# The last feed-forward of a two-layer diffusion transformer takes the residual times the norm's weights as its operand; the tokens' factors scale its up-product, and the shift is one more moving column

## The chip, the cores and the metric

The kernel runs on one core of a Trainium2 chip. A core has a matrix engine (TensorE, in the rows PE, its weight loads PEld), a vector engine (VectorE, DVE), a scalar engine (ScalarE, ACT), GpSimd (POOL) and queues that issue transfers (SP and others). Each engine works through its own queue in order and waits on semaphores for the others. Matrix products go to PSUM banks, which DVE and ACT read; everything else lies in SBUF. The metric is the time of one execution on the device, in microseconds (us).

## What is computed

There are 256 tokens and 256 context tokens of width 1024, two layers, each of a feed-forward, an attention block and a second feed-forward, all with a root-mean-square norm that is scaled and shifted by modulations. In the second layer the context's tokens end with the attention, so that its second feed-forward, the last one, has the 256 tokens alone:

```python
def _rmsnorm(x, g):
    y = x32 * lax.rsqrt(jnp.mean(x32 * x32, axis=-1, keepdims=True) + EPS)
    return (y * g.astype(jnp.float32)).astype(x.dtype)

def _modulate(h, shift, scale):
    return h * (1 + scale) + shift

def _swiglu(h, w_up, w_down):
    a, b = jnp.split(h @ w_up, 2, axis=-1)
    return (jax.nn.silu(a) * b) @ w_down

def _half_ffn(h, g, shift, scale, gate, w_up, w_down):
    return h + 0.5 * gate * _swiglu(_modulate(_rmsnorm(h, g), shift, scale), w_up, w_down)
...
        h_x = h_x + mod_x[:, :, 5] * (jnp.concatenate([o_a, o_b, o_c], axis=-1) @ w_out[l])
        h_x = _half_ffn(h_x, norm_g[l, 2], mod_x[:, :, 6], mod_x[:, :, 7], mod_x[:, :, 8], ffn2_up[l], ffn2_down[l])
```

The inner width is 2816, that is 22 chunks of 128 columns in each of the two halves a and b of the up-product.

## The kernel before

**Layout.** The residual `hT` has features on partitions: 8 chunks (index k) of 128 features, the tokens along the free dimension. Every operand of a large product is split into two float32r parts, a high part (a rounded copy) and a low part (the rest); a product is three matmuls, high by high, high by low, low by high (`mm3`, L348 to L350). An operand tile of the `act` pool (two buffers) holds both parts of all 8 chunks.

**Weights.** A stream of weight blocks comes by DMA into raw buffers (three). Each block gives two slots. `emit_split` makes a slot's high part on ACT (L306, 128x1024, or 128x768 for a part of six chunks) and its low part on DVE (L309). Seven slot buffers exist; `pump` keeps up to six or seven slots split ahead, and a next split is emitted after each slot is used up (`done`).

**Order.** Nothing reorders the program: it is emitted in the order in which each engine runs it. A clock of emitted TensorE work (`tick`, `later`) says where small steps are put among the large products: `AFTER` gives the delay of a norm's statistic and of what follows it, `ACC_LAG` that of the sums of squares.

**The boundary in question.** The second layer's `w_out_phase` calls `proj_out`: four slots of two chunks each. For every chunk of the result, DVE adds it, gated, to the residual (`resid`, L461), ACT squares it (L374) and DVE adds the squares up (L380, a chunk's sum emitted a little later). When the last chunk is out, `stat` sums over partitions by eight small matmuls (L409) and takes the reciprocal root by Newton's steps on DVE (L388 to L397); `spread` brings the tokens' factors to every partition through TensorE (L416) into PSUM; `apply` makes each chunk of the next operand from residual, weights, factors and shift:

```python
DVE.scalar_tensor_tensor(out=t, in0=hT[:, k, cols], scalar=gsc[:, i, k, v:v + 1], in1=rb[:, 0:TX], op0=ALU.mult, op1=ALU.mult)   # L436
ACT.activation(out=acol(a, k, v * TX, v * TX + TX)[0], in_=t, func=AF.Identity, bias=modT[:, l * 72 + 3 * n * 8 + k, v:v + 1])   # L437
DVE.scalar_tensor_tensor(out=al, in0=ts.pop(k), scalar=sh, in1=ah.bitcast(F32), op0=ALU.add, op1=ALU.subtract)                   # L431
```

In the second layer `flush()` emits all of that right behind `w_out_phase`, before the first product of the last feed-forward.

**The last feed-forward.** `ffn` goes through `FPARTS`, three parts of 8, 6 and 8 inner chunks. For each inner chunk there is a slot for a and one for b, 24 matmuls of 128x256 each, into a PSUM bank of its own (five banks rotate). In the first part the first four slots go together, chunk by chunk of the operand (`by_halves`). `up_evac` takes a pair of banks to a chunk of `g`, the operand of the down-product:

```python
ACT.activation(out=s[:, 0:n], in_=pa[:, 0:n], func=AF.Silu)                             # L552
DVE.tensor_tensor(out=u[:, 0:n], in0=s[:, 0:n], in1=pb[:, 0:n], op=ALU.mult)            # L555
ACT.copy(out=gh, in_=uv)                                                                # L558
DVE.tensor_tensor(out=gl, in0=uv, in1=gh.bitcast(F32), op=ALU.subtract)                 # L559
```

The silu is emitted behind the product of a, ahead of the weight split that follows it; the other three behind the product of b. After the ups of a part, `proj_out` runs eight down-slots of one output chunk each, which go through `g` chunk by chunk (24 matmuls; 18 in the part of six). In the last part each output chunk is also squared for the final norm and scaled into the result (`last_chunk`, L1265).

## Time and profile before

| what | value |
|---|---|
| time, median of three runs | 1739.68 us |
| lowest, highest | 1738.67 us, 1740.33 us |
| span of the profiled execution | 1741.7 us |
| mean granted TensorE clock | 0.987 |
| PE, DVE, ACT busy | 98%, 59%, 38% of the span |
| mean transfer rate | 142 GB/s |

The profile is of one execution, and its page gives no time of that execution other than its span from the first to the last instruction, 2.0 us above the median of the runs. Busy shares are means over stages with different limits. Matmuls overlap, so that a row's duration (0.28 us for 128x256) is longer than the distance from one to the next, and a busy PE says little about a slow one: the granted clock has to be read beside it. In a timeline row stand start, duration, engine, line, operation, result and operand, the shape, how many in a row, and in brackets the idle time of the engine before it with what ended it.

### The profile page before, as it was taken

The page shows a single profiled execution, that of the slowest core. Times are in us where ns is not written, and L with a number is a line of the kernel's source. Part 1 is how long each engine was busy: PE and PEld are TensorE (multiplying, and loading weights), DVE is VectorE, ACT ScalarE, POOL GpSimd, SP SyncE. Part 2 cuts the span into 40 slices and gives each one's busy share as a digit, 9 for nine tenths or more (in the row PEclk, how much of TensorE's full clock was granted, in tenths as well). Part 3 has the DMA queues.
Part 4 walks back from the last instruction along what each step waited for, and adds up shares of the span by engine and source line. Part 5 has one row for each costly group of instructions (what it writes and reads, how often), then busy time and mean ns, then how long its engine had stood idle before and what let it go on. Part 6 is the DMA issues. An engine that isn't in the chain of part 4 may idle for free.

```text
span 1741.7 us, 23662 instructions
## 1 busy us (share of the span) xinstructions
PE 1706.1 (98%) x9512; PEld 1428.7 (82%) x9512; DVE 1025.0 (59%) x1748; ACT 664.8 (38%) x1087; POOL 33.3 (2%) x48
## 2 busy tenths in 40 slices
PE   6999999999999999999999999999999999989998
PEld 4778888889886688888888898888888987789998
DVE  5666676566545586666664466545433656565554
ACT  4431322324545644323333243223222356554443
POOL 0000200000000000000000000020000000000000
PEclk8999999999999999999999999999999999989999
DMA  9755555431304325544653335455533133546561
GB/s 316 207 175 168 155 179 173 151 121 49 109 25 160 107 73 168 164 140 140 192 152 122 92 88 183 150 160 174 146 97 97 49 110 146 169 133 205 164 201 50
DMA packets 295335, 246.48 MB, mean 142 GB/s; under 512 B 9377, under 2 KB 262442, under 8 KB 293176
## 3 DMA queue, kind: packets, MB, share of 16 engines
q1 hardware_dynamic: 292680, 241.30, 44.7%
q0 software_dynamic: 1088, 2.15, 0.5%
q8 instruction: 75, 1.23, 0.3%
q10 hardware_dynamic: 1456, 1.52, 0.3%
q14 instruction: 36, 0.29, 0.1%
HBM read 243.88 MB, written 2.00 MB: 141 GB/s over the span
## 4 chain that ended last, share of the span: by engine, by line
PE 90%; DVE 4%; DMA 2%; ACT 2%; issue 1%; SPq 0%; DVEq 0%; ACTq 0%
PE mm L348 27%; PE mm L350 27%; PE mm L349 27%; PE mm L839 2%; PE mm L912 1%; PE aux L878 1%; PE mm L838 1%; DVE w L309 1%; PE ada L181 1%; DMA ada_raw<-in_w_ada_dram 1%; DVE ada_acc L221 1%; PE ada L229 1%; DMA raw<-in_w_ada_dram 1%; ACT w L306 1%; PE aux L409 0%
## 5 line engine op out<-in xcount | busy, mean ns | idle before, releaser
L348 PE MATMUL mm<-act,w 128*128 128x512 f32 (+1 forms) x2592 | 913.0, 352 | 5.6 <-ACT act L437 3.3
L350 PE MATMUL mm<-act,w 128*128 128x512 f32 (+1 forms) x2592 | 904.2, 349 | 1.8 <-DVE w L309 1.8
L349 PE MATMUL mm<-act,w 128*128 128x512 f32 (+1 forms) x2592 | 904.5, 349 | 1.0 <-DVE act L431 0.9
L348 PEld LDWEIGHTS mm<-act,w 128*128 128x128 f32 x2592 | 494.1, 191 | 89.3 <-issue 19.4
L350 PEld LDWEIGHTS mm<-act,w 128*128 128x128 f32 x2592 | 494.0, 191 | 64.1 <-DVE w L309 2.4
L349 PEld LDWEIGHTS mm<-act,w 128*128 128x128 f32 x2592 | 494.3, 191 | 62.5 <-DVE act L431 1.7
L309 DVE TENSOR_TENSOR w<-raw,w 128x1024 fp32r<-128x1024 f32 (+1 forms) x312 | 371.0, 1198 | 245.6 <-ACT w L306 245.2
L306 ACT CAST w<-raw 128x1024 fp32r<-128x1024 f32 (+1 forms) x312 | 314.9, 1023 | 120.4 <-PE mm L350 93.6
L221 DVE SCALAR_TENSOR_TENSOR ada_acc<-ada_raw,sc,ada_acc 128x512 f32<-128x512 f32 x308 | 216.0, 746 | 47.9 <-DMA ada_raw<-in_w_ada_dram 24.7
L558 ACT CAST act<-gf 128x512 fp32r<-128x512 f32 (+1 forms) x87 | 49.7, 571 | 318.7 <-DVE gf L555 318.7
L461 DVE SCALAR_TENSOR_TENSOR hT<-mm,hgt,hT 128x256 f32<-128x256 f32 x168 | 75.1, 480 | 97.8 <-PE mm L350 97.6
L552 ACT ACTIVATE sil<-mm 128x512 f32<-128x512 f32 (+1 forms) x87 | 47.6, 547 | 214.8 <-PE mm L350 214.5
L555 DVE TENSOR_TENSOR gf<-sil,mm 128x512 f32<-128x512 f32 (+1 forms) x87 | 54.3, 625 | 94.0 <-PE mm L350 77.7
L559 DVE TENSOR_TENSOR act<-gf,act 128x512 fp32r<-128x512 f32 (+1 forms) x87 | 54.9, 631 | 55.5 <-ACT act L558 55.5
L374 ACT ACTIVATE sq<-hT 128x256 f32<-128x256 f32 (+1 forms) x52 | 25.5, 492 | 108.4 <-DVE hT L461 108.4
L437 ACT ACTIVATE act<-nt,modT 128x256 fp32r<-128x256 f32 x88 | 43.4, 507 | 49.3 <-DVE nt L436 49.2
L219 ACT ACTIVATE ada_acc<-ada_raw,sc 128x512 f32<-128x512 f32 x44 | 29.6, 718 | 47.4 <-DMA ada_raw<-in_w_ada_dram 36.7
L855 DVE TENSOR_REDUCE nm<-mm 128x1 f32<-128x512 f32 (+1 forms) x60 | 41.0, 686 | 7.9 <-PE mm L839 7.2
L863 ACT ACTIVATE P<-mm,nm,rq 128x512 f32<-128x512 f32 (+1 forms) x48 | 33.7, 707 | 22.3 <-DVE nm L860 21.0
L431 DVE SCALAR_TENSOR_TENSOR act<-nt,modT,act 128x256 fp32r<-128x256 f32 x88 | 41.3, 480 | 1.3 <-ACT act L437 1.3
L436 DVE SCALAR_TENSOR_TENSOR nt<-hT,gsc,aux 128x256 f32<-128x256 f32 x88 | 40.8, 476 | 1.8 <-PE aux L416 1.2
L886 ACT COPY PT<-aux 128x512 f32<-128x512 f32 x60 | 32.2, 588 | 16.9 <-PE aux L878 12.9
(154 smaller groups left out, 885.5 us busy)
## 6 DMA issues: line engine op xcount, KB each, us to landing
raw<-in_ffn_up_dram SPq DMA_DIRECT2D x172, 512.0 KB
ada_raw<-in_w_ada_dram SPq DMA_DIRECT2D x192, 256.0 KB
raw<-in_ffn_down_dram SPq DMA_DIRECT2D x32, 1024.0 KB
raw<-in_w_ada_dram SPq DMA_DIRECT2D x16, 1024.0 KB
raw<-in_ffn_down_dram SPq DMA_DIRECT2D x16, 768.0 KB
raw<-in_w_in_dram SPq DMA_DIRECT2D x10, 1024.0 KB
raw<-in_w_out_dram SPq DMA_DIRECT2D x8, 1024.0 KB
raw<-in_w_ada_dram SPq DMA_DIRECT2D x12, 512.0 KB
```

Source lines behind the costliest of these rows:

```text
L221: DVE.scalar_tensor_tensor(out=o, in0=raw, scalar=col, in1=o, op0=ALU.mult, op1=ALU.add)
L306: ACT.copy(out=wh, in_=sl)
L309: DVE.tensor_tensor(out=wl, in0=sl, in1=wh.bitcast(F32), op=ALU.subtract)
L348: PE.matmul(out=ps, lhsT=wh, rhs=ah, start=start and i == 0, stop=False)
L349: PE.matmul(out=ps, lhsT=wh, rhs=al, start=False, stop=False)
L350: PE.matmul(out=ps, lhsT=wl, rhs=ah, start=False, stop=stop and i == last)
L437: ACT.activation(out=acol(a, k, v * TX, v * TX + TX)[0], in_=t, func=AF.Identity, bias=modT[:, l * 72 + 3 * n * 8 + k, v:v + 1])
L461: DVE.scalar_tensor_tensor(out=hT[:, k, cols], in0=ps, scalar=gate[:, k, v:v + 1], in1=hT[:, k, cols], op0=ALU.mult, op1=ALU.add)
L552: ACT.activation(out=s[:, 0:n], in_=pa[:, 0:n], func=AF.Silu)
L555: DVE.tensor_tensor(out=u[:, 0:n], in0=s[:, 0:n], in1=pb[:, 0:n], op=ALU.mult)
L558: ACT.copy(out=gh, in_=uv)
L559: DVE.tensor_tensor(out=gl, in0=uv, in1=gh.bitcast(F32), op=ALU.subtract)
```

## The change

The up-product of the last feed-forward is linear in its operand, and a token's factor is the same for all features. So the operand becomes the residual times the norm's weights (`gsc`), without factor and shift; the product of a token's column is multiplied by its factor afterwards; and the shift, which is the same for all tokens, is one more column of the operand, so that its product with the weights comes out as column 256 and is added as a bias. A second extra column is zero. `plain_operand` replaces `boundary` there, `last_ffn` replaces `ffn`; the `flush()` between them is dropped, and the first four slots are no longer taken together. `proj_out` and `w_out_phase` get a parameter `first`, called for each chunk between `resid` and `acc_chunk`. All other differences of the two files are comments and line numbers (one line more up to L480, five more up to L597, 91 more behind).

```diff
+NX = TX + 2
...
-    def proj_out(src, kl, ppair, gate, both, final, after, each=None):
+    def proj_out(src, kl, ppair, gate, both, final, after, each=None, first=None):
...
                 if final:
+                    if first:
+                        first(ppair * i + j)
                     acc_chunk(halves(both), ppair * i + j)
...
                     resid(ps[:, 0:TX], ch, v, gate)
+                    if first:
+                        first(ch)
                     acc_chunk((v,), ch)
...
+    def plain_operand(i):
+        l, n = divmod(i, 3)
+        shift = modT[:, l * 72 + 3 * n * 8:l * 72 + 3 * n * 8 + 8, 0:1]
+        a = {}
+
+        def chunk(k):
+            if k == 0:
+                t = actp.tile([128, 8192], F32R, tag="act", name="act")[:, 0:2 * KD * NX]
+                a["t"] = t = t.rearrange("p (s k t) -> p s k t", s=2, k=KD)
+                DVE.memset(t[:, :, :, TX + 1:NX].bitcast(F32), 0.0)
+                ACT.copy(out=t[:, 0, :, TX:TX + 1], in_=shift)
+                DVE.tensor_tensor(out=t[:, 1, :, TX:TX + 1], in0=shift, in1=t[:, 0, :, TX:TX + 1].bitcast(F32), op=ALU.subtract)
+            ah, al = acol(a["t"], k, 0, TX)
+            g = gsc[:, i, k, 0:1]
+            ACT.activation(out=ah, in_=hT[:, k, 0:TX], func=AF.Copy, scale=g)
+            DVE.scalar_tensor_tensor(out=al, in0=hT[:, k, 0:TX], scalar=g, in1=ah.bitcast(F32), op0=ALU.mult, op1=ALU.subtract)
+
+        def factors():
+            if "rb" not in a:
+                if 0 not in a:
+                    a[0] = stat(0)
+                rb = spread(0)
+                a["rb"] = tmp.tile([128, NT], F32, tag="acc", bufs=1, name="rb")[:, 0:TX]
+                ACT.copy(out=a["rb"], in_=rb[:, 0:TX])
+            return a["rb"]
+
+        def after(v):
+            def st_():
+                if 0 not in a:
+                    a[0] = stat(0)
+            later(AFTER[i][0], st_)
+            later(AFTER[i][1], factors)
+        a["factors"] = factors
+        return a, chunk, after
+
+    def last_ffn(a, gate, each):
...
+        def product(ps):
+            s = take()
+            for k in range(KD):
+                wh, wl = wcol(s, k, 0)
+                ah, al = acol(t, k, 0, NX)
+                PE.matmul(out=ps[:, 0:NX], lhsT=wh, rhs=ah, start=k == 0, stop=False)
+                PE.matmul(out=ps[:, 0:NX], lhsT=wh, rhs=al, start=False, stop=False)
+                PE.matmul(out=ps[:, 0:NX], lhsT=wl, rhs=ah, start=False, stop=k == KD - 1)
+                tick(3 * MM[TX])
+
+        def scaled(ps, name):
+            bias = small.tile([128, 8], F32, tag="nm", bufs=6, name="nm")
+            ACT.copy(out=bias[:, 0:1], in_=ps[:, TX:TX + 1])
+            o = tmp.tile([128, 512], F32, tag="t2k", bufs=T2K, name=name)[:, 0:TX]
+            DVE.tensor_tensor(out=o, in0=ps[:, 0:TX], in1=a["factors"](), op=ALU.mult)
+            return o, bias[:, 0:1]
+
+        def silu(ps):
+            o, bias = scaled(ps, "sil")
+            ACT.activation(out=o, in_=o, func=AF.Silu, bias=bias)
+            return o
+
+        def gated(s, ps, g, m):
+            o, bias = scaled(ps, "gf")
+            DVE.scalar_tensor_tensor(out=o, in0=o, scalar=bias, in1=s, op0=ALU.add, op1=ALU.mult)
+            gh, gl = acol(g, m, 0, TX)
+            ACT.copy(out=gh, in_=o)
+            DVE.tensor_tensor(out=gl, in0=o, in1=gh.bitcast(F32), op=ALU.subtract)
+
+        for pi, (f0, nf) in enumerate(FPARTS):
+            g = act_tile()
+            for m in range(nf):
+                pa, pb = mm_bank(), mm_bank()
+                product(pa)
+                s = silu(pa) if "rb" in a else None
+                done()
+                product(pb)
+                s = silu(pa) if s is None else s
+                gated(s, pb, g, m)
+                done()
+            proj_out(lambda k, lo, hi, g=g: acol(g, k, lo, hi), nf, 1, gate, False, pi == 2, lambda v: None, each if pi == 2 else None)
...
-            nxt2, after2 = boundary(3 * l + 2)
-            w_out_phase(l, O, both, after2)
-            if not both:
-                flush()
             if l == 0:
+                nxt2, after2 = boundary(3 * l + 2)
+                w_out_phase(l, O, both, after2)
                 a, after3 = boundary(3)
                 ffn(nxt2, hgt[:, 1], True, after3, True, None, MODS[1])
             else:
-                ffn(nxt2, hgt[:, 3], False, lambda v: None, True, None, (), last_chunk)
+                nxt2, chunk, after2 = plain_operand(5)
+                w_out_phase(l, O, both, after2, chunk)
+                last_ffn(nxt2, hgt[:, 3], last_chunk)
```

How this moves instructions shows at three places. First DVE's queue at the end of w_out. Names: `hT` the residual, `acc` and `sq` the sum of squares and a chunk's squares, `w<-raw` a weight split's low part. From the residual of chunk 4 to the first step of the statistic, before:

```order
L309 TENSOR_TENSOR w<-raw,w 128x1024 x2
L461 SCALAR_TENSOR_TENSOR hT<-mm,modT,hT 128x256
L380 TENSOR_TENSOR acc<-acc,sq 128x256 x2
L461 SCALAR_TENSOR_TENSOR hT<-mm,modT,hT 128x256
L380 TENSOR_TENSOR acc<-acc,sq 128x256
L461 SCALAR_TENSOR_TENSOR hT<-mm,modT,hT 128x256
L380 TENSOR_TENSOR acc<-acc,sq 128x256
L461 SCALAR_TENSOR_TENSOR hT<-mm,modT,hT 128x256
L380 TENSOR_TENSOR acc<-acc,sq 128x256
L388 TENSOR_SCALAR rs_v<-aux 128x2
```

And of the changed kernel, the same stretch, where `act<-hT,gsc,act` is the low part of an operand's chunk:

```order
L310 TENSOR_TENSOR w<-raw,w 128x1024 x2
L462 SCALAR_TENSOR_TENSOR hT<-mm,modT,hT 128x256
L619 SCALAR_TENSOR_TENSOR act<-hT,gsc,act 128x256
L381 TENSOR_TENSOR acc<-acc,sq 128x256 x2
L462 SCALAR_TENSOR_TENSOR hT<-mm,modT,hT 128x256
L619 SCALAR_TENSOR_TENSOR act<-hT,gsc,act 128x256
L381 TENSOR_TENSOR acc<-acc,sq 128x256
L462 SCALAR_TENSOR_TENSOR hT<-mm,modT,hT 128x256
L619 SCALAR_TENSOR_TENSOR act<-hT,gsc,act 128x256
L381 TENSOR_TENSOR acc<-acc,sq 128x256
```

The operand's low parts, which stood behind the statistic as L431, now stand between a chunk's residual and its sum of squares.

Second, TensorE's queue behind w_out's last matmul. `aux<-ones,acc` and `aux<-ones,sq` are the statistic, `aux<-ident,rs_y` the spreading of the factors. Before:

```order
L350 MATMUL mm<-act,w 128x256
L409 MATMUL aux<-ones,acc 128x1 x2
L409 MATMUL aux<-ones,sq 128x1 x2
L416 MATMUL aux<-ident,rs_y 128x128 x2
L348 MATMUL mm<-act,w 128x256
```

And of the changed kernel, around the statistic; the first three rows are the third such triple behind w_out's last matmul:

```order
L649 MATMUL mm<-act,w 128x258
L650 MATMUL mm<-act,w 128x258
L651 MATMUL mm<-act,w 128x258
L410 MATMUL aux<-ones,acc 128x1 x2
L410 MATMUL aux<-ones,sq 128x1 x2
L649 MATMUL mm<-act,w 128x258
```

Nine matmuls of the first up-slot, three chunks of the operand, now stand ahead of the statistic, and the spreading (not shown) stands fifteen matmuls into the second slot.

Third, one pair of up-slots in the middle of a part. DVE before (`gf<-sil,mm` is silu times b, `act<-gf,act` the low part of `g`):

```order
L555 TENSOR_TENSOR gf<-sil,mm 128x256
L559 TENSOR_TENSOR act<-gf,act 128x256
L309 TENSOR_TENSOR w<-raw,w 128x1024 x2
```

DVE of the changed kernel (`rb` holds the factors, `nm` the bias, `sil` and `gf` the scaled products of a and b):

```order
L659 TENSOR_TENSOR sil<-mm,rb 128x256
L310 TENSOR_TENSOR w<-raw,w 128x1024
L659 TENSOR_TENSOR gf<-mm,rb 128x256
L669 SCALAR_TENSOR_TENSOR gf<-gf,nm,sil 128x256
L672 TENSOR_TENSOR act<-gf,act 128x256
L310 TENSOR_TENSOR w<-raw,w 128x1024
```

ACT before and of the changed kernel, for the same pair:

```order
L552 ACTIVATE sil<-mm 128x256
L306 CAST w<-raw 128x1024
L558 CAST act<-gf 128x256
L306 CAST w<-raw 128x1024
```

```order
L657 COPY nm<-mm 128x1
L664 ACTIVATE sil<-sil,nm 128x256
L307 CAST w<-raw 128x1024
L657 COPY nm<-mm 128x1
L671 CAST act<-gf 128x256
L307 CAST w<-raw 128x1024
```

Before, ACT's silu read the PSUM bank; now it reads DVE's product of that bank, which stands in DVE's queue behind the low part of the weight split before it.

More of the change, by code (lines that the diff above doesn't have):

```diff
@@ new lines, in last_ffn @@
+    def last_ffn(a, gate, each):
+        st["ffn"] += 1
+        st["urgent"] = None
+        t = a["t"]
+        def product(ps):
[35 more added lines that the diff above has]
+            proj_out(lambda k, lo, hi, g=g: acol(g, k, lo, hi), nf, 1, gate, False, pi == 2, lambda v: None, each if pi == 2 else None)
@@ L1098, in attention, with w_out_phase @@
         return O[0]
-    def w_out_phase(l, O, both, after):
+    def w_out_phase(l, O, both, after, first=None):
         gate = modT[:, l * 72 + 40:l * 72 + 48, :]
-        proj_out(lambda k, lo, hi: acol(O, 4 + k, lo, hi), 4, 2, gate, both, True, after)
+        proj_out(lambda k, lo, hi: acol(O, 4 + k, lo, hi), 4, 2, gate, both, True, after, None, first)
     ada_all = [[(g, k) for k in range(KD)] for g in range(9)]
```

## The prediction

> **What bounds the kernel now.** I read the page first (the span and the chain that ended last), then the last 240 us by stretches, and then the timeline of TensorE, VectorE (DVE) and ScalarE (ACT) around the one place where TensorE stands still.
>
> ```profile
> span 1741.7 us, 23662 instructions
> PE 90%; DVE 4%; DMA 2%; ACT 2%; issue 1%; SPq 0%; DVEq 0%; ACTq 0%
> ```
>
> TensorE is 90% of the chain: time is won only where it waits and lost wherever something new makes it wait. The stretches around the last feed-forward (busy time by engine, granted clock, DMA share, GB/s):
>
> ```profile
> 1516.80:1520.20 3.40, 3.40 (x19) 3.40 (x18) 3.40 (x4) 1.72 (x2) 0.00 (x0) 0.51 0.04 9
> 1528.60:1537.90 9.30, 2.51 (x11) 2.07 (x10) 5.97 (x23) 2.23 (x6) 0.00 (x0) 0.60 0.41 113
> 1537.90:1544.20 6.30, 6.30 (x28) 6.07 (x29) 5.18 (x11) 4.26 (x7) 0.00 (x0) 0.50 0.01 3
> 1552.60:1731.20 178.60, 178.54 (x1488) 178.34 (x1487) 102.47 (x133) 80.33 (x118) 0.00 (x0) 1.00 0.54 160
> ```
>
> The second row is the norm's wait, 9.3 us with 2.5 us of matmul work. The third is its echo: full work at clock 0.50, 28 matmuls in 6.30 us (0.225 each). The last row is the steady feed-forward: 1488 matmuls of 128x256 in 178.6 us, 0.120 each, no gap; DVE 57% and ACT 45% busy. The wait itself, from the timeline:
>
> ```profile
> 1515.73 0.38 PE L348 MATMUL mm<-act,w 128*128 128x256 f32 x1 [1.66 <-ACT act L924]
> 1526.13 2.36 DVE L309 TENSOR_TENSOR w<-raw,w 128x1024 fp32r<-128x1024 f32 x2 [1.43 <-ACT w L306]
> 1528.34 0.28 PE L350 MATMUL mm<-act,w 128*128 128x256 f32 x1
> 1528.41 0.48 DVE L461 SCALAR_TENSOR_TENSOR hT<-mm,modT,hT 128x256 f32<-128x256 f32 x1
> 1531.44 0.41 DVE L380 TENSOR_TENSOR acc<-acc,sq 128x256 f32<-128x256 f32 x1
> 1532.00 0.98 PE L409 MATMUL aux<-ones,acc 128*128 128x1 f32 x4 [3.39 <-DVE acc L380]
> 1532.85 0.99 PE L409 MATMUL aux<-ones,sq 128*128 128x1 f32 x4
> 1536.13 0.66 PE L416 MATMUL aux<-ident,rs_y 128*128 128x128 f32 x2 [2.29 <-DVE rs_y L397]
> 1537.90 0.58 PE L348 MATMUL mm<-act,w 128*128 128x256 f32 x1 [1.11 <-ACT act L437]
> 1552.26 0.60 ACT L552 ACTIVATE sil<-mm 128x512 f32<-128x512 f32 x1 [4.24 <-PE mm L350]
> ```
>
> w_out's last product ends at 1528.5, but VectorE, busy splitting weights until 1528.4, is three chunks behind: residual of chunk 4 at 1528.41, last sum of squares at 1531.85. Then the statistic (1532.0 to 1533.84), Newton's steps, the spreading, the first operand chunk: 1537.90. The first four up-slots (96 matmuls) are done at 1552.1, where ACT takes them.
>
> **Prices.** By form, from 1500 us on (count, busy, mean ns of one, idle before):
>
> ```profile
> L306 ACT CAST w<-raw 128x1024 fp32r<-128x1024 f32 x64 | 66.0, 1043 | 17.9 <-PE mm L350 17.9
> L306 ACT CAST w<-raw 128x768 fp32r<-128x768 f32 x8 | 6.4, 828 | 0.0
> L558 ACT CAST act<-gf 128x256 fp32r<-128x256 f32 x20 | 8.1, 406 | 40.7 <-DVE gf L555 40.7
> L552 ACT ACTIVATE sil<-mm 128x256 f32<-128x256 f32 x20 | 7.6, 382 | 25.3 <-PE mm L350 25.2
> L437 ACT ACTIVATE act<-nt,modT 128x256 fp32r<-128x256 f32 x8 | 4.0, 507 | 8.9 <-DVE nt L436 8.9
> L1265 ACT ACTIVATE res<-hT,colsB 128x256 f32<-128x256 f32 x8 | 3.9, 493 | 0.0
> L552 ACT ACT_TABLE_LOAD x1 | 1.3, 1283 | 0.0
> L863 ACT ACTIVATION_READ_ACCUMULATOR P<-mm,nm,rq 128x1 f32 x2 | 0.4, 190 | 0.0
> L309 DVE TENSOR_TENSOR w<-raw,w 128x1024 fp32r<-128x1024 f32 x64 | 77.5, 1222 | 41.6 <-ACT w L306 41.6
> L309 DVE TENSOR_TENSOR w<-raw,w 128x768 fp32r<-128x768 f32 x8 | 7.7, 956 | 4.7 <-ACT w L306 4.7
> L555 DVE TENSOR_TENSOR gf<-sil,mm 128x256 f32<-128x256 f32 x20 | 8.4, 420 | 6.9 <-PE mm L350 6.9
> L559 DVE TENSOR_TENSOR act<-gf,act 128x256 fp32r<-128x256 f32 x20 | 8.5, 425 | 9.4 <-ACT act L558 9.4
> L431 DVE SCALAR_TENSOR_TENSOR act<-nt,modT,act 128x256 fp32r<-128x256 f32 x8 | 3.8, 480 | 0.4 <-ACT act L437 0.4
> ```
>
> One pair of up-slots in the steady state, DVE and ACT:
>
> ```profile
> 1575.66 0.42 DVE L555 TENSOR_TENSOR gf<-sil,mm 128x256 f32<-128x256 f32 x1 [0.31 <-PE mm L350]
> 1576.12 0.41 ACT L558 CAST act<-gf 128x256 fp32r<-128x256 f32 x1 [2.02 <-DVE gf L555]
> 1576.43 1.04 ACT L306 CAST w<-raw 128x1024 fp32r<-128x1024 f32 x1
> 1577.51 1.23 DVE L309 TENSOR_TENSOR w<-raw,w 128x1024 fp32r<-128x1024 f32 x1 [0.52 <-ACT w L306]
> 1578.54 0.38 ACT L552 ACTIVATE sil<-mm 128x256 f32<-128x256 f32 x1 [1.07 <-PE mm L350]
> 1578.82 1.04 ACT L306 CAST w<-raw 128x1024 fp32r<-128x1024 f32 x1
> 1579.89 1.23 DVE L309 TENSOR_TENSOR w<-raw,w 128x1024 fp32r<-128x1024 f32 x1 [1.16 <-ACT w L306]
> 1581.42 0.42 DVE L555 TENSOR_TENSOR gf<-sil,mm 128x256 f32<-128x256 f32 x1 [0.30 <-PE mm L350]
> ```
>
> The pair repeats every 5.76 us (1575.66 to 1581.42: 48 matmuls). A handoff costs 0.04 (1576.08 to 1576.12, 1577.47 to 1577.51). Two ACT instructions in a row overlap by 0.10 (1576.12 + 0.41 against 1576.43), two of DVE by 0.08 (2.36 for two of 1.22). Each engine now reaches its next step before TensorE needs it.
>
> **The change, part by part.** *The operand.* Eight pairs of DVE steps (L436, L431) and eight of ACT (L437) leave the path after the norm; eight scaled copies (ACT, as L1265: 0.49) and eight low parts (DVE, as L431: 0.48) go in among w_out's residuals. In DVE's queue a chunk is now residual, low part, sum, and the low part waits for ACT in between: 0.48 + 0.04 + 0.49 + 0.04 + 0.40 + 0.34 = 1.79 us. In the two slots before chunk 4 the second residual starts 1.07 later and its copy stands ahead of ACT's next weight cast (0.41): 1.48 each, so chunk 4's residual moves from 1528.41 to 1531.4. Four chunks at 1.79 and one more sum (0.46) put the last sum's end at 1539.0 instead of 1531.85.
>
> *The statistic in TensorE's queue.* It now stands behind nine up-matmuls, which end by about 1530.1. It starts at 1539.15, ends 1.84 later (as before) at 1541.0, and 87 of the 96 matmuls remain. The factors come while they run, so the old waits of 2.29 and 1.11 us are covered; but TensorE has been still for 9.0 us first. The clock after such a wait was 0.50 for 6.30 us, after the 1.66 us wait at 1515.73 for about 3.4 (first row of the stretches). With 3.1 us slow: 14 matmuls, 73 more at 0.121, spreading 0.3: 1553.2. With 6.3 us slow: 1554.7. Against 1552.1 that is **+1.1 to +2.6; I take +1.8**, the middle. The gain wished for at this place is gone: it is paid in VectorE's queue.
>
> *Two more columns.* 128x512 matmuls stand 0.227 apart:
>
> ```profile
> 1196.83 0.39 PE L350 MATMUL mm<-act,w 128*128 128x512 f32 x1
> 1198.19 0.39 PE L350 MATMUL mm<-act,w 128*128 128x512 f32 x1
> ```
>
> (six steps in 1.36). A straight line from 0.120 at 256 gives 0.0008 for two columns; 1056 such matmuls: **+0.8** (bounds: nothing, and what 512 columns cost, which is a rival below; two columns are nearest to the former).
>
> *The evacuation, and this is the main term.* Per pair, DVE gets a third step (product a by the factors, product b by the factors, then b plus shift times silu) and ACT's silu, formerly released by TensorE, now waits for DVE's product a. That closes a circle through both in-order queues: a's product 0.42 + 0.04; silu, now with a bias from SBUF as L437, 0.51 - 0.10; weight cast 1.04 + 0.04; split 1.22 - 0.08; b's product 0.42 + 0.04; sum and product 0.48 + 0.04; cast of the result 0.41 - 0.10; weight cast 1.04 + 0.04; split 1.22 - 0.08. Sum **6.60 us against 5.80** that TensorE takes for 48 matmuls. The copies of the one column (44, some 0.2 as the smallest ACT row) fall where ACT waits anyway. DVE and ACT are far from full, but they take turns. Five PSUM banks and six split slots let TensorE run on while they fall behind, so the debt is due where a part ends: the first down-slot needs the last chunk.
>
> Part 3 (8 pairs), counted from the end of the first product: a's product of pair 2 starts at 6.9 instead of 5.8 (column copy 0.24 and one round), pair 8's at 6.9 + 6 x 6.60 = 46.5, and its low part is out 4.95 later (0.46 + 0.41 + 1.08 + 1.14 + 0.46 + 0.52 + 0.45 + 0.43, the last from L559): 51.45. TensorE is at that chunk at 15 x 2.90 + 7 x 0.36 = 46.0. With a handoff and a weight load: 5.6 us of standing still. Part 2 (6 pairs) splits the narrower down weights from pair 4 on; their circle is 6.60 - 2 x (0.215 + 0.266) = 5.64, so the debt stops growing: 6.9 + 2 x 6.60 + 2 x 5.64 + 4.47 = 35.9 against 11 x 2.90 + 5 x 0.36 = 33.7, 2.2 us. Part 1 starts late, because the factors reach SBUF only about when pair 1's products end: a's product follows 0.8 later, behind DVE's last split (ACT's table load, 1.28, runs beside), the rest of the round takes 0.46 + 0.41 + 0.24 + 0.46 + 0.52 + 0.31 + 1.08 + 1.14 = 4.6, so pair 2's product begins 5.4 after them and 2.5 after its bank is full (2.9), not 1.1: 5.6 + 1.4 = 7.0. **Sum +14.8.**
>
> *The clock behind these waits.* A slow stretch of 3.4 us costs 0.47 of it, 1.6 us; one of 6.3 costs 2.9. For 7.0 and 5.6 us of waiting I take 2.2 each (1.6 to 2.9), for 2.2 us 1.0 (0 to 1.6): **+5.4**. The nearest row is the 1.66 us wait, which did lower the clock. The Trainium skill (TensorE: Matmul & The Clock Gate, section "Why this matters for your kernels") asks for idle gaps above about 3 us before the clock drops; the trace does not agree, as a gap of 1.66 us brought 3.4 us at 0.51. By the page the 2.2 us wait would be free and the sum 1.0 lower.
>
> Edits at nothing: the DMA queue issues the same rows in the same order, and loads only start later when splits do, with a DMA share of 0.54 to catch up in; the factors' tile takes the buffer of the sums of squares, free by then; the end of the program (statistic, turning, output) is untouched.
>
> **Sum:** 1.8 + 0.8 + 14.8 + 5.4 = +22.8 us on a profiled span of 1741.7; the page gives that execution no other time. The span stands 2.0 us (0.1%) above the median of the runs, 1739.7, to which I add the difference: **1762**.
>
> **Rivals.**
> - *The circle doesn't bind* (steps overlap better than their sum, 5.80 or less): only the boundary and the columns remain, 1739.7 + 2.6 = 1742, within 0.2%. For it: DVE 57%, ACT 45%. Against: each link above has a row. 0.07. A circle of about 6.1 would leave some 1743.5 to 1752: 0.06.
> - *Faster.* The operand's chunks slip into VectorE's idle times (1.43 us before the splits at 1526.13), the last sum ends near 1531.9 as now, and the nine matmuls plus the covered waits count: restart at 1533.9, 87 x 0.121 + 0.3 + 2.2 for the slow clock gives 1546.9 instead of 1552.1, and with no circle 1739.7 - 5.2 + 0.8 = 1735. It decides at a last sum before 1537.2 and a circle under 5.80; both are needed. 0.05.
> - *258 columns are dear.* If each cost as much as 512 columns do, 1056 x 0.107 = 113 us, with the circle hidden: 1854. Nothing in this trace has an odd width or a pitch of 1032 bytes, so 0.04.
> - Forecast: 0.78.
>
> **Range and chances.** Low: silu at the 0.38 of L552 and the last step at 0.42 take 0.19 off the circle (3.4 in all), no slow clock at the parts' ends (5.4), 1.1 at the boundary (0.7): 13.3, so 1753. High: handoffs of 0.10 in the five places (0.3 a pair, 5.4 in all), slow clocks at their upper ends (2.0) and 2.6 at the boundary (0.8): 31, so 1771. I give 1752 to 1771. 0.2%, 3.5 us, is about what a measurement here can tell from no change: faster 0.05, same 0.07, slower 0.88.
>
> **What would show it.** In the profile after: last sum of squares some 7 us later and a wait of TensorE of 8 to 10 us at the statistic, behind nine matmuls; pairs of up-slots at 5.8 us on TensorE, but products on DVE 6.6 apart; three waits in the first down-slot of each part, about 7, 2 and 5.5 us, put down to the low part of the gated product; clock 0.5 after them; 258-wide matmuls 0.121 apart. Wrong if those three waits are missing (then the circle was mis-sized) or if the statistic starts before 1537.

## The result, and the profile after

The changed kernel takes 1761.5 us (median of four runs, 1760.5 to 1762.4) against 1740.0 for the kernel before on the same chip: 1.0127 times the time, 95% interval 1.0112 to 1.0141. The prediction was 1762, between 1752 and 1771, slower with a chance of 0.88.

The page after, first lines of the span and of the chain that ended last:

```profile
span 1760.3 us, 23693 instructions
PE 83%; DVE 7%; ACT 5%; DMA 2%; issue 2%; SPq 0%; ACTq 0%; DVEq 0%
```

TensorE's share of the chain falls from 90% to 83%, and DVE's and ACT's together rise from 6% to 12%: the chain now runs through those two for a longer part of its way. The waits from 1500 us on say where (engine and line, what it waited for, us in total, times, longest):

```profile
PE mm L349 <- ACT act L671: 12.4, 3, 5.6
PE aux L410 <- DVE acc L381: 10.5, 2, 9.6
```

The first row is new. L349 is the first matmul of a triple in a down-slot, L671 the high part of the gated product: three times TensorE stands before the last chunk of a part. The second row is, but for 0.9 us, the boundary's wait, now in one piece. It ends with the last sum of squares on DVE and the statistic on TensorE:

```profile
1538.20 0.42 DVE L381 TENSOR_TENSOR acc<-acc,sq 128x256 f32<-128x256 f32 x1
1538.76 0.98 PE L410 MATMUL aux<-ones,acc 128*128 128x1 f32 x4 [9.56 <-DVE acc L381]
```

Stretch by stretch (columns as in the prediction: busy time by engine, granted clock, DMA share, GB/s):

```profile
1529.30:1538.90 9.60, 0.14 (x1) 0.17 (x2) 6.98 (x15) 4.33 (x10) 0.00 (x0) 0.71 0.43 115
1538.90:1544.00 5.10, 5.10 (x26) 5.10 (x27) 3.12 (x13) 2.00 (x3) 0.00 (x0) 0.55 0.00 0
1552.60:1749.60 197.00, 184.49 (x1490) 183.13 (x1488) 115.31 (x171) 83.79 (x157) 0.00 (x0) 0.97 0.49 145
1595.80:1602.00 6.20, 6.20 (x29) 6.03 (x30) 3.15 (x5) 2.78 (x4) 0.00 (x0) 0.54 0.57 158
1657.40:1664.00 6.60, 6.52 (x53) 6.33 (x54) 5.26 (x8) 4.17 (x5) 0.00 (x0) 1.00 0.75 203
1727.20:1734.00 6.80, 6.80 (x41) 6.62 (x42) 3.53 (x5) 3.43 (x7) 0.00 (x0) 0.70 0.01 2
```

The third row answers to the last row of stretches in the prediction: 178.6 us for 1488 matmuls before, 197.0 us for 1490 now, though DVE is busy for 115 us of it and ACT for 84, neither nearly full. The rows below it are what follows each of the three waits: 29 matmuls in 6.2 us at clock 0.54, then 53 in 6.6 us at full clock, then 41 in 6.8 us at 0.70.

The three waits on TensorE, from the timeline:

```profile
1595.76 0.58 PE L349 MATMUL mm<-act,w 128*128 128x256 f32 x1 [5.60 <-ACT act L671]
1657.31 0.38 PE L349 MATMUL mm<-act,w 128*128 128x256 f32 x1 [1.73 <-ACT act L671]
1727.08 0.58 PE L349 MATMUL mm<-act,w 128*128 128x256 f32 x1 [5.07 <-ACT act L671]
```

And what makes them, a pair of up-slots on DVE:

```profile
1551.78 0.42 DVE L659 TENSOR_TENSOR sil<-mm,rb 128x256 f32<-128x256 f32 x1
1553.71 1.23 DVE L310 TENSOR_TENSOR w<-raw,w 128x1024 fp32r<-128x1024 f32 x1 [1.51 <-ACT w L307]
1554.86 0.42 DVE L659 TENSOR_TENSOR gf<-mm,rb 128x256 f32<-128x256 f32 x1
1555.31 0.48 DVE L669 SCALAR_TENSOR_TENSOR gf<-gf,nm,sil 128x256 f32<-128x256 f32 x1
1556.27 0.43 DVE L672 TENSOR_TENSOR act<-gf,act 128x256 fp32r<-128x256 f32 x1 [0.47 <-ACT act L671]
1557.22 1.22 DVE L310 TENSOR_TENSOR w<-raw,w 128x1024 fp32r<-128x1024 f32 x1 [0.53 <-ACT w L307]
1558.37 0.42 DVE L659 TENSOR_TENSOR sil<-mm,rb 128x256 f32<-128x256 f32 x1
```

From one product of a by the factors (`sil<-mm,rb`) to the next: 6.59 us. In each round DVE stands 1.51 + 0.47 + 0.53 = 2.5 us waiting for ACT, and ACT in turn for DVE. TensorE needs 5.77 for the same pair, so each pair leaves some 0.8 us of debt, and the part's end collects it.

To compare runs free of what lies ahead, I use the stretch from the start of w_out's first matmul to that of the last down-slot's last one. It is read off rows like these, of the changed kernel:

```profile
1515.23 0.39 PE L349 MATMUL mm<-act,w 128*128 128x256 f32 x1 [1.66 <-ACT act L1015]
1749.54 0.28 PE L351 MATMUL mm<-act,w 128*128 128x256 f32 x1
```

That is 234.3 us; before it is 215.1 (1515.73 to 1730.86): +19.2 in this pair of profiles.

### The profile page after: what moved, and what is told of

Read it like the earlier page. It is cut to its first block, busy times and chain, and to the rows that moved or that the text cites. A ratio compares the mean times of both kernels' runs of the same rounds, so it can differ in the third digit from the quotient of the medians.

```text
span 1760.3 us, 23693 instructions
## 1 busy us (share of the span) xinstructions
PE 1710.1 (97%) x9512; PEld 1431.2 (81%) x9512; DVE 1039.8 (59%) x1788; ACT 671.1 (38%) x1135; POOL 33.3 (2%) x48
## 3 DMA queue, kind: packets, MB, share of 16 engines
q8 instruction: 75, 1.23, 0.3%
## 4 chain that ended last, share of the span: by engine, by line
PE 83%; DVE 7%; ACT 5%; DMA 2%; issue 2%; SPq 0%; ACTq 0%; DVEq 0%
PE mm L349 24%; PE mm L350 24%; PE mm L351 24%; DVE w L310 3%; ACT w L307 3%; PE mm L930 2%; PE mm L1003 1%; PE aux L969 1%; PE mm L929 1%; PE ada L182 1%; DMA ada_raw<-in_w_ada_dram 1%; DVE ada_acc L222 1%; ACT sil L664 1%; PE ada L230 1%; DVE gf L669 1%
## 5 line engine op out<-in xcount | busy, mean ns | idle before, releaser
L349 PE MATMUL mm<-act,w 128*128 128x512 f32 (+1 forms) x2240 | 814.8, 364 | 16.9 <-ACT act L671 12.4
L350 PE MATMUL mm<-act,w 128*128 128x512 f32 (+1 forms) x2240 | 806.8, 360 | 1.1 <-DVE act L432 0.9
L351 PE MATMUL mm<-act,w 128*128 128x512 f32 (+1 forms) x2240 | 805.4, 360 | 1.9 <-DVE w L310 1.9
L349 PEld LDWEIGHTS mm<-act,w 128*128 128x128 f32 x2240 | 427.4, 191 | 101.1 <-issue 19.4
L563 ACT CAST act<-gf 128x512 fp32r<-128x512 f32 x66 | 41.0, 621 | 275.6 <-DVE gf L560 275.6
L557 ACT ACTIVATE sil<-mm 128x512 f32<-128x512 f32 x66 | 39.4, 597 | 184.1 <-PE mm L351 184.0
L649 PE MATMUL mm<-act,w 128*128 128x258 f32 x352 | 100.6, 286 | 0.0
L650 PE MATMUL mm<-act,w 128*128 128x258 f32 x352 | 99.9, 284 | 0.0
L651 PE MATMUL mm<-act,w 128*128 128x258 f32 x352 | 99.9, 284 | 0.0
L560 DVE TENSOR_TENSOR gf<-sil,mm 128x512 f32<-128x512 f32 x66 | 45.2, 686 | 80.3 <-PE mm L351 69.6
L564 DVE TENSOR_TENSOR act<-gf,act 128x512 fp32r<-128x512 f32 x66 | 45.7, 693 | 45.3 <-ACT act L563 45.3
L438 ACT ACTIVATE act<-nt,modT 128x256 fp32r<-128x256 f32 x80 | 39.5, 507 | 41.3 <-DVE nt L437 41.2
```

Of the source, the lines that this page charges most:

```text
L349: PE.matmul(out=ps, lhsT=wh, rhs=ah, start=start and i == 0, stop=False)
L350: PE.matmul(out=ps, lhsT=wh, rhs=al, start=False, stop=False)
L351: PE.matmul(out=ps, lhsT=wl, rhs=ah, start=False, stop=stop and i == last)
L649: PE.matmul(out=ps[:, 0:NX], lhsT=wh, rhs=ah, start=k == 0, stop=False)
L650: PE.matmul(out=ps[:, 0:NX], lhsT=wh, rhs=al, start=False, stop=False)
L651: PE.matmul(out=ps[:, 0:NX], lhsT=wl, rhs=ah, start=False, stop=k == KD - 1)
```

## The experiments

Two theories stood against each other. The first: the *order* in which evacuation and weight split stand in DVE's and ACT's queues makes a round trip of 6.6 us, and its debt is the loss. The second: the added *work* on these two engines makes it, in whatever order. Besides these, the boundary or the two columns could carry the loss. The expectations count a wait from the start of one matmul to the next, less one spacing, so that 5.8, 1.9 and 5.2 there are the 5.60, 1.73 and 5.07 above. The medians, each against runs of the kernel before on the same chip (1739.6 for the first four, 1740.8 for the other four), with the stretch just defined:

| kernel | median us | ratio, 95% interval | stretch us, against 215.1 |
|---|---|---|---|
| changed | 1761.5 | 1.0127, 1.0112 to 1.0141 | 234.3, +19.2 |
| queue order alone | 1743.7 | 1.0026, 1.0015 to 1.0036 | 216.4, +1.3 |
| dependency cut | 1743.1 | 1.0018, 1.0007 to 1.0028 | 216.4, +1.3 |
| boundary alone | 1742.8 | 1.0014, 1.0001 to 1.0027 | 217.3, +2.1 |
| evacuation alone | 1762.0 | 1.0125, 1.0106 to 1.0145 | 234.1, +19.0 |
| one product less | 1747.2 | 1.0041, 1.0027 to 1.0056 | 223.3, +8.2 |
| 256 columns | 1762.4 | 1.0134, 1.0118 to 1.0149 | 234.3, +19.1 |
| low part later | 1739.1 | 0.9992, 0.9982 to 1.0001 | 214.1, -1.0 |
| norm covered | 1733.3 | 0.9959, 0.9947 to 0.9972 | 206.6, -8.6 |

**Queue order alone.** `emit_split` has a place between its ACT cast and its DVE subtraction; the evacuation goes there.

```diff
+        def done_with(fn):
+            st["out"] -= 1
+            if st["out"] < st["look"] and next_main():
+                emit_split(fn)
+            else:
+                fn()
+            pump()
...
-                s = silu(pa) if "rb" in a else None
-                done()
+                done_with(lambda: s.append(silu(pa)) if "rb" in a else None)
...
-                gated(s, pb, g, m)
-                done()
+                done_with(lambda: gated(s[0], pb, g, m))
```

> The same instructions as in the changed kernel; only the order in which the evacuation and the weight split stand in the queues of ACT and DVE is changed: the cast of the next weights is put ahead of the evacuation on ACT, and the low part of these weights behind the evacuation on DVE. If the order of the two queues makes the round trip of 6.6 us (theory), the low part of the weights no longer stands between the first product by the factors and the second one, the trip falls below the 5.80 us of TensorE, the waits of 5.8, 1.9 and 5.2 us ahead of the parts' first down-slots are gone, and with them the slow stretches behind the first and the third (about 4.3 us in all): 1761.5 - 13.0 - 4.3 = 1744 us, 1742 to 1746. If the amount of work on DVE and ACT makes it (rival), nothing changes: 1760 to 1763.

Measured: 1743.7. The stretch of the up- and down-slots and the products of a on DVE:

```profile
1552.60:1731.60 179.00, 178.92 (x1490) 178.65 (x1488) 113.53 (x171) 87.03 (x156) 0.00 (x0) 1.00 0.54 159
1552.14 0.42 DVE L659 TENSOR_TENSOR sil<-mm,rb 128x256 f32<-128x256 f32 x1
1557.02 0.42 DVE L659 TENSOR_TENSOR sil<-mm,rb 128x256 f32<-128x256 f32 x1
1561.90 0.42 DVE L659 TENSOR_TENSOR sil<-mm,rb 128x256 f32<-128x256 f32 x1
1567.44 0.42 DVE L659 TENSOR_TENSOR sil<-mm,rb 128x256 f32<-128x256 f32 x1
1573.19 0.42 DVE L659 TENSOR_TENSOR sil<-mm,rb 128x256 f32<-128x256 f32 x1
```

1490 matmuls in 179.0 us where the changed kernel has 197.0; 171 instructions on DVE in both. The round is 4.88 us while DVE catches up with the late start (1552.14, 1557.02, 1561.90), then 5.5 and 5.75, which is TensorE's pace. With all the work still there, the loss falls from 19.2 us to 1.3, of which 0.7 stand at the boundary: the order makes the long round, the amount of work alone does not.

**Dependency cut.** The products stay as many and as long, but silu reads the bank ahead of DVE's product, whose result is not used.

```diff
-            o, bias = scaled(ps, "sil")
-            ACT.activation(out=o, in_=o, func=AF.Silu, bias=bias)
-            return o
+            bias = small.tile([128, 8], F32, tag="nm", bufs=6, name="nm")
+            ACT.copy(out=bias[:, 0:1], in_=ps[:, TX:TX + 1])
+            s = tmp.tile([128, 512], F32, tag="t2k", bufs=T2K, name="sil")[:, 0:TX]
+            ACT.activation(out=s, in_=ps[:, 0:TX], func=AF.Silu, bias=bias[:, 0:1])
+            o = tmp.tile([128, 512], F32, tag="t2k", bufs=T2K, name="idle")[:, 0:TX]
+            DVE.tensor_tensor(out=o, in0=ps[:, 0:TX], in1=a["factors"](), op=ALU.mult)
+            return s
```

> DVE's product of the gate's bank by the factors is still made, into a tile that nobody reads, and silu reads the bank itself, ahead of it (the factor of the gate is left out). DVE and ACT have as many instructions of the same lengths as in the changed kernel. Theory: silu no longer waits for a DVE that stands behind a weight split, so one crossing of the two queues leaves the round trip; it falls below 5.80 us, the three waits and the slow clock behind them are gone: 1742 to 1746. Rival, load: 1760 to 1763. Rival, the second product is what matters: half of the 17 us goes, about 1753.

Measured: 1743.1, the same stretch of 216.4 us; none of the three waits is left. One crossing between the queues less is as good as the other order, with as many instructions as before (silu, which reads the bank here, takes 0.48 us instead of 0.51).

**Boundary alone.** Operand, columns and late statistic of the change, evacuation of before:

```diff
-            o, bias = scaled(ps, "sil")
-            ACT.activation(out=o, in_=o, func=AF.Silu, bias=bias)
+            o = tmp.tile([128, 512], F32, tag="t2k", bufs=T2K, name="sil")[:, 0:TX]
+            ACT.activation(out=o, in_=ps[:, 0:TX], func=AF.Silu)
...
-            o, bias = scaled(ps, "gf")
-            DVE.scalar_tensor_tensor(out=o, in0=o, scalar=bias, in1=s, op0=ALU.add, op1=ALU.mult)
+            o = tmp.tile([128, 512], F32, tag="t2k", bufs=T2K, name="gf")[:, 0:TX]
+            DVE.tensor_tensor(out=o, in0=s, in1=ps[:, 0:TX], op=ALU.mult)
```

> The changed operand, its two further columns and the late statistic, with the evacuation of before: silu from the bank, its product with the up-bank, and no factors and no shift (both are left out of the result; the factors are still computed). Theory: only the boundary's +1.1 and the columns' +0.8 remain: 1740.0 + 1.9 = 1742, 1741 to 1744. Rival, the boundary carries most of the loss: over 1750. Rival, the boundary gains what the change wanted and the evacuation hid it: under 1738.

Measured: 1742.8, 0.14% over before. Of the +2.1 us in the stretch, 1.9 stand ahead of the fifth up-slot. The boundary neither gains nor carries the loss.

**Evacuation alone.** The kernel before, with the changed kernel's evacuation from the third pair on and a tile of ones for the factors:

```diff
+            o = tmp.tile([128, 512], F32, tag="t2k", bufs=T2K, name=name)[:, 0:TX]
+            DVE.tensor_tensor(out=o, in0=ps[:, 0:TX], in1=scaled_by["ones"], op=ALU.mult)
...
+        ACT.activation(out=s, in_=s, func=AF.Silu, bias=bias)
```

> The kernel before, with its boundary and its normed operand of 256 columns, and in the last feed-forward from the third pair of up-slots on the changed kernel's evacuation: a column copy, a product by a tile of ones, silu or the gated product from that (the copied column is the last token's, so that the result is another). Theory: the round trip is 6.6 us again and the waits ahead of the down-slots come back at about their size (in part 1 two pairs fewer, so some 4 to 6 instead of 5.8; 2 and 5 in parts 2 and 3), with the slow clock behind them: 1740.0 + 12.0 + 4.3 = 1756, 1753 to 1760. Rival, the boundary carries the loss: 1740 to 1743.

Measured: 1762.0, two us over the range: the whole loss, without the new boundary and without the columns. In part 1, DVE and TensorE:

```profile
1552.33 4.63 DVE L309 TENSOR_TENSOR w<-raw,w 128x1024 fp32r<-128x1024 f32 x4 [0.26 <-ACT w L306]
1557.34 0.42 DVE L553 TENSOR_TENSOR sil<-mm,rb 128x256 f32<-128x256 f32 x1
1563.93 0.42 DVE L553 TENSOR_TENSOR sil<-mm,rb 128x256 f32<-128x256 f32 x1
1588.16 0.38 PE L348 MATMUL mm<-act,w 128*128 128x256 f32 x1 [1.75 <-ACT act L562]
1594.73 0.58 PE L348 MATMUL mm<-act,w 128*128 128x256 f32 x1 [5.60 <-ACT act L562]
```

The round is 6.59 us here too. I had reckoned with six pairs of debt from an even start. But here four weight splits stand in one piece ahead of the first product (4.63 us), so the debt is already there when the rounds begin, and part 1 waits twice in its first down-slot, one round apart, for the last chunk but one (1.75 us) and for the last (5.60). That the total meets the changed kernel's so closely is in part chance: the three parts lose 21.0 us here, against 18.4 in the changed kernel, and the boundary, which this kernel shares with the kernel before, took 2.0 us less in this profile than in that one (from w_out's first matmul to the fifth up-slot's 34.7 us against 36.7).

**One product less.** If the debt is a sum over the pairs, a shorter round must shrink the waits in proportion.

```diff
-            o, bias = scaled(ps, "gf")
-            DVE.scalar_tensor_tensor(out=o, in0=o, scalar=bias, in1=s, op0=ALU.add, op1=ALU.mult)
+            bias = small.tile([128, 8], F32, tag="nm", bufs=6, name="nm")
+            ACT.copy(out=bias[:, 0:1], in_=ps[:, TX:TX + 1])
+            o = tmp.tile([128, 512], F32, tag="t2k", bufs=T2K, name="gf")[:, 0:TX]
+            DVE.scalar_tensor_tensor(out=o, in0=ps[:, 0:TX], scalar=bias[:, 0:1], in1=s, op0=ALU.add, op1=ALU.mult)
```

> The changed kernel without the up-bank's product by the factors (left out of the result): the gated product reads the bank itself, so that one DVE instruction of 0.42 us a pair is gone from the round trip and nothing else. Theory: the round trip falls from 6.59 to about 6.15 us, still over 5.80; the debt grows by 0.35 instead of 0.79 us a pair, so the waits ahead of the down-slots are 5.8 - 7 x 0.44 = 2.7, none and 5.2 - 3.1 = 2.1 us instead of 5.8, 1.9 and 5.2, and of the slow clock behind them (4.3 us) a part stays: 1744 + 4.8 + 0 to 3 = 1750, 1748 to 1753. Rival, the waits have a fixed cause that isn't the sum of a debt over the pairs: 1757 or more.

Measured: 1747.2, a little under the range. Two rounds on DVE, the waits at L349 (total, times, longest), and the stretch behind the first of them:

```profile
1551.42 0.42 DVE L659 TENSOR_TENSOR sil<-mm,rb 128x256 f32<-128x256 f32 x1
1557.54 0.42 DVE L659 TENSOR_TENSOR sil<-mm,rb 128x256 f32<-128x256 f32 x1
1563.66 0.42 DVE L659 TENSOR_TENSOR sil<-mm,rb 128x256 f32<-128x256 f32 x1
PE mm L349 <- ACT act L673: 3.5, 2, 2.1
1592.20:1599.00 6.80, 6.72 (x41) 6.53 (x42) 4.59 (x6) 3.83 (x4) 0.00 (x0) 0.75 0.70 187
```

The round is 6.12 us. The waits are 2.1 and 1.4 us, part 2's is gone, and the clock is low behind the first alone. Counted as in the expectation they are 2.3 and 1.5 us where I expected 2.7 and 2.1. They fell somewhat further, but as a debt over pairs does, and not as a fixed cause would.

**256 columns.**

```diff
-NX = TX + 2
+NX = TX
...
-            ACT.copy(out=bias[:, 0:1], in_=ps[:, TX:TX + 1])
+            ACT.copy(out=bias[:, 0:1], in_=ps[:, TX - 1:TX])
```

> The changed kernel with 256 moving columns in the last feed-forward: no shift and no zero column (the shift is left out of the result; the column copy reads the bank's last column). Matmuls 0.120 us apart instead of 0.1208. Theory: 1056 matmuls by 0.0008 us = 0.85 us less, and the faster TensorE pays it back in longer waits, as the round trip of 6.6 us sets the time in the up-slots: 1761, 1760 to 1762. Rival, the odd width costs more than its spacing shows: below 1758.

Measured: 1762.4, 0.4 over the range, and the interval overlaps that of the changed kernel. The rival is out, but the theory's reason isn't borne out either: the waits are not longer (5.61, 1.73 and 5.04 us). There was hardly anything to win, as the changed kernel shows in part 1, between the first matmul of the fifth up-slot and that of the first down-slot:

```profile
1552.60 0.28 PE L649 MATMUL mm<-act,w 128*128 128x258 f32 x1
1587.19 0.28 PE L349 MATMUL mm<-act,w 128*128 128x256 f32 x1
```

These 288 matmuls of 258 columns take 34.59 us, 0.1201 each, not 0.1208. So two columns more cost some 0.1 us in all 1056 matmuls.

**Low part later.** On top of the queue order, a chunk's low part goes behind the next chunk's residual:

```diff
-            ah, al = acol(a["t"], k, 0, TX)
-            g = gsc[:, i, k, 0:1]
-            ACT.activation(out=ah, in_=hT[:, k, 0:TX], func=AF.Copy, scale=g)
-            DVE.scalar_tensor_tensor(out=al, in0=hT[:, k, 0:TX], scalar=g, in1=ah.bitcast(F32), op0=ALU.mult, op1=ALU.subtract)
+            ACT.activation(out=acol(a["t"], k, 0, TX)[0], in_=hT[:, k, 0:TX], func=AF.Copy, scale=gsc[:, i, k, 0:1])
+            late(k)
+
+        def late(k):
+            if k:
+                ah, al = acol(a["t"], k - 1, 0, TX)
+                DVE.scalar_tensor_tensor(out=al, in0=hT[:, k - 1, 0:TX], scalar=gsc[:, i, k - 1, 0:1], in1=ah.bitcast(F32), op0=ALU.mult, op1=ALU.subtract)
...
+            late(KD)
```

> The queue order of the experiment before (1743.7 us), and the operand's low part of a chunk emitted behind the residual of the next chunk, so that DVE no longer stands 0.58 us a chunk behind ACT's high part. Theory: from w_out's end DVE takes some 1.2 instead of 1.79 us a chunk, four chunks in a row, so the sums of squares and the statistic come 2.3 us earlier and the wait of 9.84 us ahead of the statistic is 7.5: 1743.7 - 2.3 = 1741.4, 1740 to 1743. Rival, the statistic waits for something else (the weight splits at 1528.6, the residuals' matmuls): 1743 to 1745.

Measured: 1739.1, 0.9 under the range and 1.7 under the kernel before, where the queue order alone was 4.1 over it; in the stretch it is 2.3 less than the queue order alone. Two residuals on DVE, the statistic on TensorE, and what follows it:

```profile
1530.10 0.48 DVE L462 SCALAR_TENSOR_TENSOR hT<-mm,modT,hT 128x256 f32<-128x256 f32 x1
1531.22 0.48 DVE L462 SCALAR_TENSOR_TENSOR hT<-mm,modT,hT 128x256 f32<-128x256 f32 x1
1533.24 0.98 PE L410 MATMUL aux<-ones,acc 128*128 128x1 f32 x4 [6.08 <-DVE acc L381]
1533.00:1541.60 8.60, 8.36 (x41) 8.39 (x42) 5.37 (x15) 2.38 (x3) 0.00 (x0) 0.54 0.08 22
```

A chunk takes 1.12 us, and the wait falls from 9.56 to 6.08, by 3.5 us where 2.3 were expected. The slow stretch behind it is longer in this profile, 8.6 us at 0.54 with the statistic in it, and takes 1.2 of it back. The time is that of the kernel before (the interval has 1 in it): what the queue order left of the loss is about what the low parts cost where the change put them.

**Norm covered.** Both of these, and the statistic is put where TensorE has other work. Of the diff, the first four up-slots:

```diff
+        def first_pair():
+            sl = [take(), take()]
+            ps = [mm_bank() for _ in range(4)]
+            for i, k in [(i, k) for i in range(2) for k in range(4)] + [(i, k) for k in range(4, KD) for i in range(2)]:
...
+            emit_split()
+            add_squares()
+            emit_split()
+            product(ps[2])
+            a["stat"]()
+            product(ps[3])
+            emit_split()
+            emit_split()
+            a["factors"]()
+            return ps
```

> The order of the queues and the late low parts of the two experiments before; also, the first two up-slots are taken chunk by chunk of the operand, the third and the fourth are multiplied before any factor is needed (four banks), the statistic stands behind the third slot on TensorE and the spread behind the fourth, the sums of squares stand behind the last chunk's low part on DVE. Theory: the wait of 9.84 us ahead of the statistic and the one for the spread are covered by matmuls that need no factors; about 1.1 us is left, for the second slot's weights; of the slow stretch that follows the wait (10 us at half clock, some 4 us lost) nothing is left; the first evacuation starts later, and 1 us of it may show at the first part's down-slots: 1743.7 - 8.7 - 4 + 1 = 1732, 1729 to 1737, faster than both kernels. Rival, DVE's and ACT's work at w_out's end has to be done anyway and comes back as waits in part 1: 1740 or more.

Measured: 1733.3, faster than the kernel before by 0.41% (0.28 to 0.53) and some 28 us faster than the changed one. The one wait left at the boundary, the statistic without a wait, the two stretches from there, and what is left of the waits in the down-slots:

```profile
1525.53 0.38 PE L693 MATMUL mm<-act,w 128*128 128x258 f32 x1 [0.69 <-DVE act L630]
1533.28 0.58 PE L414 MATMUL aux<-ones,acc 128*128 128x1 f32 x4
1525.60:1540.00 14.40, 14.38 (x119) 14.20 (x120) 12.17 (x30) 8.76 (x17) 0.00 (x0) 1.00 0.54 148
1540.00:1717.00 177.00, 176.41 (x1465) 175.73 (x1464) 115.14 (x175) 87.30 (x159) 0.00 (x0) 1.00 0.55 161
PE mm L349 <- ACT act L682: 0.4, 1, 0.4
```

The norm's wait is 0.7 us in place of 9.6 (for the low part of a chunk, not for the second slot's weights, as I had thought), and the clock stays at 1.00 from there to the end of the last down-slot. The rival, that DVE's and ACT's work comes back as waits in part 1, is out: 0.4 us of idle time is left in the down-slots, which take 1.5 us longer than those of the kernel before, while the place ahead of them gains 10.2 (from w_out's first matmul to the fifth up-slot's 26.5 us instead of 36.7).

## Why the prediction was right

By its own steps, in the profiled pair:

- **The round.** 6.60 us worked out, 6.59 measured, and in the round that starts at 1551.78 each link is within 0.02 us of its term. The runs show that this chain is the cause: another order, or one dependency less, each changed alone with the work left as it is, removes all three waits.
- **The waits.** Predicted 7.0, 2.2 and 5.6 us, measured 5.60, 1.73 and 5.07: 12.4 in place of 14.8. Two steps were off. The prediction lets a wait end with the low part of the last chunk, but it ends with the high part (`<-ACT act L671`), which in part 1 is out at 1595.70, the low part at 1596.16; the second matmul of the triple then waits some 0.3 us more. And in part 1 a's product of the first pair was to follow 0.8 us behind the end of the pair's matmuls. It starts 0.6 ahead of it (1546.40 against 1546.99), but ACT's table load, which was to run beside, stands between it and silu (1546.38 to 1547.66). So pair 2's product starts 4.8 us behind the end of pair 1's matmuls instead of 5.4.
- **The clock behind the waits.** Predicted 2.2, 1.0 and 2.2. At 0.120 a matmul the three stretches shown would be 3.5, 6.4 and 4.9 us instead of 6.2, 6.6 and 6.8: 2.7, 0.2 and 1.9, in all 4.8 against 5.4. The middle term was wrong: 1.73 us of waiting left the clock at 1.00 (why, stands in the last section). The Trainium skill (TensorE: Matmul & The Clock Gate, section "Why this matters for your kernels"), by whose rule that wait would be free, was right there; at w_out's start a wait of 1.66 us lowered it, in the changed kernel as before.
- **The boundary.** Predicted +1.8 and a wait of 9.0 us; the wait was 9.56, the last sum of squares ended at 1538.6 (1539.0 predicted). Counted from w_out's first matmul, the fifth up-slot's first matmul comes 0.7 us later (1552.42 - 1515.73 before, 1552.60 - 1515.23 now). That is less than predicted, because of the two slow stretches that the prediction reckoned with it was the short one (13 slow matmuls behind the statistic, 14 taken: +1.1), and because the fifth slot of the kernel before starts at 1552.42 and not at 1552.1. With the long one the same place comes 1.9 us later (boundary alone) and 1.8 (one product less), so the predicted middle lies between two cases that both occur.
- **The columns.** Predicted +0.8, measured some +0.1: the spacing is 0.1201, where the straight line to 512 columns gave 0.1208. This term was mis-sized.

The stretch's +19.2 is 0.7 at the boundary, 0.1 for the columns and 18.4 in the down-slots of the three parts (8.8, 2.3 and 7.3), where waits of 12.4 and slow clock of 4.8 are the main part and the rest is small: each wait is 0.16 longer from matmul to matmul, and the low parts of the chunks keep TensorE for some tenths. The predicted sum, 22.8, was thus 3.6 too high: 1.1 at the boundary, 0.7 for the columns, 1.8 in the waits and the clock behind them. It met the measured difference of the medians, 21.5, in part by chance. In every run on record the span is some 1.8 us shorter than the time, so that the profiled execution of the kernel before, with its span of 1741.7, took some 1743.4 us by estimate, 3.4 above the median, where that of the changed kernel (1762.1) was 0.6 above its own. The spans of the two differ by only 18.7; the 2.8 us between that and 21.5 are these 3.4 less 0.6.

## What to carry to other kernels

Two engines that are each half busy can still set the pace when a result crosses between their in-order queues several times a round: add up the chain of crossings, queue neighbours included, and compare it with the round of the engine that they serve. Where it is longer, look at what stands between two crossings before taking work away; here the same instructions in another order went from 6.59 to 4.88 us a round. And a step taken off the critical path saves only if the steps put in its place don't delay the next thing in the same queue.

## What the runs showed of the hardware

The length of a wait alone did not decide about the clock. Waits of 1.38, 1.73 and 1.75 us in the down-slots left it at 1.00. The wait of 1.66 us at w_out's start was followed by a slow stretch in every kernel here, and so was one of 2.11 us in a down-slot (0.75 over 6.8 us). The traces show what made the difference. In each of them the granted clock changes on a grid of 3.41 us: the slow stretches from w_out to the last down-slot last 3.41, 6.83, 10.24 or 13.65 us, which are whole multiples of it. Where the grid lies differs from trace to trace: its first point behind the start of w_out's first matmul comes 0.22 to 1.23 us after it, though the same instructions stand ahead of it in all ten kernels. Two pairs of neighbouring grid intervals of the changed kernel (columns as above, the clock third from the end):

```profile
1512.79:1516.21 3.42, 1.68 (x12) 1.28 (x11) 1.66 (x5) 2.38 (x6) 0.00 (x0) 1.00 0.20 49
1516.21:1519.62 3.41, 3.41 (x18) 3.41 (x18) 3.41 (x4) 1.92 (x3) 0.00 (x0) 0.50 0.02 5
1652.74:1656.15 3.41, 2.84 (x24) 2.63 (x22) 2.11 (x4) 1.29 (x3) 0.00 (x0) 1.00 0.40 118
1656.15:1659.57 3.42, 2.18 (x16) 1.99 (x17) 2.61 (x6) 2.61 (x4) 0.00 (x0) 1.00 0.72 189
```

The wait of 1.66 us lies inside one interval, in which TensorE is busy for 1.68 of 3.42 us, and the next interval is slow. The wait of 1.73 us is cut in two by a grid point; TensorE is busy for 2.84 us of the one interval and 2.18 of the other, and the clock stays. From the interval with w_out's start to the last down-slot, in all ten traces, an interval at full clock in which TensorE was busy for up to 0.51 of the time was followed by a slow one, with one exception (0.47, evacuation alone, at 1526.11), and one with 0.61 or more was not.

The grid also set how long the slow stretch behind the boundary's wait was. Seven kernels have the statistic behind nine matmuls. In four of them (changed kernel, queue order, dependency cut, 256 columns) the first grid point came 1.34 to 1.60 us after the statistic's start, and the clock returned at the second. In three (boundary alone, one product less, low part later) the first came after 0.59 to 0.85 us, and the clock returned only at the third. Behind waits of the same 9.6 us the long stretch cost 1.1 to 1.4 us more, which is as much as the boundary's terms. A difference of this size between two single profiles need not be one between the kernels. What sets the place of the grid, these runs do not show.
